# Four unused strips of 32 to 224 bytes that move where tiles begin in on-chip memory

## The chip, the cores and the metric

The kernel runs on one core of a Trainium2 chip. The metric is device time in microseconds (us) of one execution. Before the change, three runs gave a median of 1342.72 us (1341.16 to 1344.79). The profile is of one more execution of the same program.

The core has a matrix engine (PE; its weight loads are listed as PEld), a vector engine (DVE), an activation engine (ACT), GpSimd (POOL) and a queue engine (SP) that here only issues DMAs. On-chip memory has 128 partitions; "a tile begins at byte b" means byte b within every partition.

## The reference

One layer of a diffusion backbone over 256 latent tokens and 256 context tokens of width 2048, all in float32:

```python
h  = modulate(rmsnorm(x,  norm1_g), sh1, sc1)       # shifts and scales: silu(c) @ ada_w + ada_b
hc = modulate(rmsnorm(xc, norm1_g), csh1, csc1)
q, k, v, f, hy = split_projection(h @ w_in)         # 2048 -> 1024+1024+1024+512+1536
kc, vc = split(hc @ w_in[:, 1024:3072])
a = neighbourhood_attention(q, k, v, kc, vc, rpb)   # 8 heads of 128
y = merge_groups(a, fourier_mix(f), hyena_mix(hy, ...), mix_norm_g)
x = x + g1 * (y @ w_out)                            # 2048 x 2048
x = x + g2 * conv_gated_mlp(modulate(rmsnorm(x, norm2_g), sh2, sc2), ...)   # d_ff 5632
return rmsnorm(x, final_norm_g)
```

## The kernel before

Activations lie transposed: features on the 128 partitions, the 256 tokens along the row. A tile of 16 feature blocks is 16 rows of 256 float32, so one block is 1024 bytes in each partition.

**A main product takes three matmuls.** Weights and activations are split in two parts, hi (rounded to fp32r) and lo (the rest): `split` (L166) and `shift_split` (L238). `mm3` (L158) then adds hi·hi, hi·lo and lo·hi into one PSUM bank. Each of them is one MATMUL with one LDWEIGHTS ahead of it. The operand that is loaded by LDWEIGHTS is 128 columns (512 bytes) and is called stationary here; the operand that streams through is called moving. In the names of the profile the moving operand stands first: `acc_ps<-h_hi,w_hi` streams `h_hi` past a loaded `w_hi`.

In nearly all main products the activation is the moving operand, 256 columns or 1024 bytes of a row, and the weight is stationary. Only for the values of attention (the second half of `group`, L539) is it the other way: there a weight of 512 columns streams past a loaded activation.

**The weights** come from HBM in pieces of 128 x 1024 float32 into eight `raw` buffers (`Weights.load`, L248, on SP's queue), are split by ACT (hi) and DVE (lo) into two buffers each of `w_hi` and `w_lo`, and each such pair serves 48 matmuls (48 or 96 in the key and value stage). `Stream` (L272) asks for a chunk ahead of its use. Beside that, `pump` (L342) puts weight columns of the modulation through DVE (L333), in places given by a table.

**The stages**, in order:

- Key and value stage (L583 to L597): norms, the first modulation rows (L466, `s_t` stationary side of a small product), and keys and values of latent and context tokens. `group` alternates 48 matmuls on `hx_hi`, `hx_lo` (latent) with 48 on `hc_hi`, `hc_lo` (context), from the same weight buffers.
- Other input projections (L684 to L774): Fourier, Hyena and query columns, by `wide` on `hx_hi`, `hx_lo`, with the Fourier and Hyena mixing between them.
- Attention and output projection (L784 to L847): `yB_hi`, `yB_lo`, `yA_hi`, `yA_lo` are moving.
- Feed-forward part (L849 to L910): the up products on `h2_hi`, `h2_lo` (in the profile `h_hi`, `h_lo`), 4224 matmuls, and the down products on `yh`, `yl`, 2112 matmuls; then the last norm and the output.

**Where tiles lie.** Every pool is a contiguous piece of the partition. Pools on the right side are stacked downward from the top, so a strip in an early one moves every later one down too, until a pool is closed and its place given back. The `rot` pool at the top holds `hx_hi` (tag A, later `xr`), `kT` (tag C, later `h2_hi`) and `v_t` (tag D, later `h2_lo`). Below it lie, one after the other in time: `x_lo` (the tiles `hx_lo`), `hy`, `p1` (with `hc_hi`), `c_lo` (with `hc_lo`); later `fourier`, `hyena`, `att` (with `yA` and `yB`) and `ffn` (with `yh`, `yl`). The weight buffers lie on the left side.

Of the kernel before, what the change touches and what calls it, by code (L numbers as in the profile page):

```python
# [8 lines left out]
F32 = mybir.dt.float32  # L9
# [6 lines left out]
P = 128  # L16
# [19 lines left out]
for _n, _k in V_LAYOUT:  # L36
# [10 lines left out]
    p1=(0, 0, 2, 6, 9),  # L47
    blocks=(2, 2, 4, 4, 4),
    win=0.8,
    att=(1, 0, 1, 4, 0, 1, 0, 0),  # L50
# [12 lines left out]
    wa=(1, 2, 0, 0, 0, 1, 0, 0),  # L63
    outs=(2, 4, 4, 4, 2),
)


def kv_blocks():
# [55 lines left out]
def hybrid_block(ctx: ExitStack, tc: tile.TileContext, a: dict, out: bass.AP):  # L124
# [5 lines left out]
    def pool(stack, name, bufs=1, side=None, **kw):  # L130
        return stack.enter_context(tc.tile_pool(name=name, bufs=bufs, side=side, reuse_waits="tile", **kw))

    acc_ps = pool(ctx, "acc_ps", 5, space=PSUM)
    mi_ps = pool(ctx, "mi_ps", 3, space=PSUM)

    def bank(p=None):
        p = p or mi_ps
# [63 lines left out]
    def rms_bcast(pool_, sqs, n, name, ps=None):  # L201
        if ps is None:
            ps = bank()
            col_sums(ps, sqs)
        ms = pool_.tile([P, 2], F32, name=f"{name}_m", tag=f"{name}_m")
        TS(ms[:], ps[:, 0:2], 1.0 / n, EPS, op0=ALU.mult, op1=ALU.add)
        r = rstd_of(pool_, ms[:], 2, name)
        ps = bank()
        for t in range(2):
            dg = cst.tile([P, P], F32, tag="dg", name="dg", bufs=2)  # L210
            TS(dg[:], ident, r[:, t : t + 1], None, op0=ALU.mult)
            mm(ps[:, t * P : (t + 1) * P], ones[:], dg[:], True, True)
        rb = pool_.tile([P, L], F32, name=f"{name}_b", tag=f"{name}_b")
        nc.vector.tensor_copy(rb[:], ps[:, :L])
        return rb
# [73 lines left out]

    w1 = Weights(ctx, 8, 2)  # L290

    rot = pool(ctx, "rot", 1, "right")

    def rtile(tag, shape, dt, name):
# [57 lines left out]
    p1 = pool(p1s, "p1", 1, "right")  # L352
# [2 lines left out]
    s_t = p1.tile([P, KT, 32], F32, name="s_t")  # L355
    nc.gpsimd.memset(s_t[:], 0.0)
    hc_hi = p1.tile([P, KT, L], F32R, name="hc_hi")
    hc_lo = Pairs(c_pool, F32R, "hc_lo")
    hs = ((hx_hi, hx_lo), (hc_hi, hc_lo))
    xs = [Pairs(z, F32, "x_in", KT // 2) for z in (x_pool, c_pool)]  # L360
# [323 lines left out]
    with ExitStack() as st:  # L684
        fp = pool(st, "fourier", 1, "right")
# [98 lines left out]
    with ExitStack() as st:  # L784
        ap_ = pool(st, "att", 1, "right")
        yA_hi, yA_lo = (ap_.tile([P, 8, L], F32R, name=f"yA_{z}") for z in ("hi", "lo"))
        aT = ap_.tile([P, NH, L], F32, name="aT")
        yB_hi = ap_.tile([P, 8, L], F32R, name="yB_hi")
        yB_lo = ap_.tile([P, 8, L], F32R, name="yB_lo")
        for i in range(0, 8, 2):  # L790
            split(yB_hi[:, i : i + 2, :], yB_lo[:, i : i + 2, :], yB[:, i : i + 2, :])
        sqa = ap_.tile([P, L], F32, name="sqA")
        held = {}
        x_parts = []

        def wout_chunk(h, n, kc):
            yh, yl = ((yB_hi, yB_lo), (yA_hi, yA_lo))[h]
            if kc == 0:
                held[n] = [bank(acc_ps) for _ in range(2)]
            wide_chunk(stream, h * 8 + n * 2 + kc, held[n], yh, yl, kc * 4, kc == 0, kc == 1, h * kc == 1 and n == 3)  # L800
            if kc == 1:
                add_scaled(held[n], n, G1)
            if h == 1:
                pump(CFG["wa"][2 * n + kc])
            if h == 1 and kc == 1:
                square_parts(ap_, n, x_parts, "PT", 2)

        scale = 128.0 ** -0.5
        for hd in range(NH):
            PT = ap_.tile([P, 4, L], F32, tag="PT", name="PT", bufs=2)  # L810
            for t in range(2):
                ps = bank(acc_ps)
                mm(ps[:], qT[:, hd, t * P : (t + 1) * P], kT[:, hd, :], True, True)
                s = ap_.tile([P, 512], F32, tag="s", name="s", bufs=3)
                STT(s[:, :L], ps[:, :L], scale, bias[:, hd, 2 - 2 * t : 6 - 2 * t, :].rearrange("p m c -> p (m c)"), op0=ALU.mult, op1=ALU.add)
                nc.scalar.activation(s[:, L:], ps[:, L:], AF.Copy, scale=scale)
                sm = ap_.tile([P, 3], F32, tag="sm", name="sm", bufs=3)
                nc.vector.tensor_reduce(sm[:, 0:1], s[:], axis=AX.X, op=ALU.max, negate=True)
                nc.scalar.activation(s[:], s[:], AF.Exp, bias=sm[:, 0:1], accum_out=sm[:, 1:2])
                nc.vector.reciprocal(sm[:, 2:3], sm[:, 1:2])  # L820
                TS(s[:], s[:], sm[:, 2:3], None, op0=ALU.mult)
                ps = bank()
                for j in range(4):
                    transpose(ps[:, j * P : (j + 1) * P], s[:, j * P : (j + 1) * P])
                nc.scalar.copy(PT[:, :, t * P : (t + 1) * P], ps.rearrange("p (j n) -> p j n", n=P))  # L825
            ps = bank()
            for j in range(4):
                mm(ps[:, :L], v_t[:, j, hd * P : (hd + 1) * P], PT[:, j, :], j == 0, j == 3)
            nc.scalar.copy(flip(aT[:, hd, :]), ps[:, :L].rearrange("p (r c) -> p r c", c=GW))
            square_into(ap_, sqa, aT[:, hd, :], hd == 0)  # L830
            for c in range(CFG["pace"][hd], CFG["pace"][hd + 1]):
                wout_chunk(0, c // 2, c % 2)
            pump(CFG["att"][hd])
        group_norm(ap_, [aT[:, i, :] for i in range(NH)], V_MIX, yA_hi, yA_lo, 0, [sqa])
        for c in range(CFG["pace"][NH], 8):
            wout_chunk(0, c // 2, c % 2)
        for n in range(4):
            for kc in range(2):
                wout_chunk(1, n, kc)
        pump(CFG["rest"])  # L840
        rb2 = rms_bcast(ap_, x_parts, D, "r2")
        STT(A2[:], A2[:], 1.0, vec[:, V_N2 : V_N2 + KT], op0=ALU.add, op1=ALU.mult)
        h2_hi = rtile("C", [P, KT, L], F32R, "h2_hi")
        h2_lo = rtile("D", [P, KT, L], F32R, "h2_lo")
        for k in range(KT):
            t = modulate(ap_, xr[:, k, :], A2[:, k : k + 1], rb2[:])
            shift_split(t, B2[:, k : k + 1], h2_hi[:, k, :], h2_lo[:, k, :])  # L847
# [14 lines left out]
    for kind, g in plan:  # L862
        if kind == "up":
            if g == 0:
                pss = [bank(acc_ps) for _ in range(4)]
                for kc in range(4):
                    for m in range(2):
                        wide_chunk(stream, ci + 2 * kc + m, pss[2 * m : 2 * m + 2], h2_hi, h2_lo, kc * 4, kc == 0, kc == 3)
                gates, upps = pss[:2], pss[2:]
            else:  # L870
                gates = wide(stream, ci, h2_hi, h2_lo)
            gls = []
            for h in range(2):
                ga = fp.tile([P, 2, L], F32, tag="ga", name="ga", bufs=3)
                for i in range(2):
                    nt = g * 4 + 2 * h + i
                    wv = [vec[:, V_FCW + 44 * q + nt : V_FCW + 44 * q + nt + 1] for q in range(3)]
                    conv(gates[h][:, i * L : (i + 1) * L], ga[:, i, :], *wv, vec[:, V_FCB + nt : V_FCB + nt + 1])
                nc.scalar.activation(ga[:], ga[:], AF.Gelu_apprx_tanh)
                gls.append(ga)  # L880
            if g:
                upps = wide(stream, ci + 4, h2_hi, h2_lo)
            ci += 8
            yh = fp.tile([P, 4, L], F32R, tag="yh", name="yh", bufs=6)
            yl = fp.tile([P, 4, L], F32R, tag="yl", name="yl", bufs=6)
            for h in range(2):
                TT(gls[h][:], upps[h].rearrange("p (i n) -> p i n", n=L), gls[h][:], op=ALU.mult)
                split(yh[:, 2 * h : 2 * h + 2, :], yl[:, 2 * h : 2 * h + 2, :], gls[h][:])
            ys[g] = (yh, yl)
        else:  # L890
            if g == 0:
                pump(99)
            gs = halves[g]
            for n in range(4):
                pss = [bank(acc_ps) for _ in range(2)]
                for q in gs:
                    wide_chunk(stream, ci, pss, *ys[q], 0, q == gs[0], q == gs[-1], g == 1 and n == 3 and q == gs[-1])
                    ci += 1
                add_scaled(pss, n, G2)
                if g == 1:  # L900
                    square_parts(fp, n, f_parts, "ga2", 1)
                    for c in range(4 * n, 4 * n + 4):
                        nc.scalar.activation(xr[:, c, :], xr[:, c, :], AF.Copy, scale=vec[:, V_FG + c : V_FG + c + 1])
    rb = rms_bcast(fp, f_parts, D, "rf")
    c0 = 0
    for n in CFG["outs"]:
# [91 lines left out]
```

## Time and profile before

| | |
|---|---|
| median of three runs | 1342.72 us |
| the profiled execution | 1340.31 us |
| its span, first to last instruction | 1338.5 us |
| mean granted TensorE clock | 0.986 |
| PE busy | 1311.0 us, 10302 matmuls |
| DVE busy | 890.7 us |
| ACT busy | 555.7 us |
| mean rate of the DMAs | 234 GB/s |

A PE that is listed as busy says little here: a matmul of 256 columns is listed with about 280 ns, but the next begins after some 115 to 120 ns, since matmuls overlap. What counts is the time from the start of one matmul to the start of the next, called the interval below. It is read from the chain of work that ended last (a piece's length by its number of matmuls), from the timeline (starts of single matmuls), or from a stretch of time by the number of matmuls that touch it.

### The profile page before, as it was taken

Reading aid. Unit: us, or ns where it says so; the run is one execution under the profiler, and the core shown is the slowest. Engines: PE = TensorE matmul, PEld = TensorE weight load, DVE = VectorE, ACT = ScalarE, POOL = GpSimd, SP = SyncE. Lnnn points to the kernel's source line nnn. Section 1 sums busy time; section 2 is a strip of 40 time slices with the busy share of each in tenths; the row PEclk is TensorE's granted clock in tenths of the full one; section 3 lists DMA queues with packets and bytes.
Section 4 is the critical chain, followed back from the end, with each engine's and each line's share of the span. In section 5 each row is a group of like instructions: output and inputs, shape, how many; then the busy total and the mean of one; then the engine's idle time right before and its main releaser. Section 6 shows DMA issues by size and latency. Waiting matters only on the chain.

```text
span 1338.5 us, 24519 instructions
## 1 busy us (share of the span) xinstructions
PE 1311.0 (98%) x10302; PEld 1235.1 (92%) x10302; DVE 890.7 (67%) x1305; ACT 555.7 (42%) x735; POOL 0.9 (0%) x7
## 2 busy tenths in 40 slices
PE   9899999999999999989999999999999999999996
PEld 5677788899989889989999999999999999999996
DVE  5347668958999998877666767644445554555653
ACT  4252212135334665455443444333334443443542
POOL 0000000000000000000000000000000000000000
PEclk9799999999999999989999999999999999999997
DMA  8677888987669775746777777855555555565531
GB/s 322 248 303 284 329 325 306 339 274 275 214 235 343 286 232 184 275 139 223 251 245 260 246 246 248 280 183 186 189 188 189 190 186 192 184 194 183 188 135 64
DMA packets 93311, 313.18 MB, mean 234 GB/s; under 512 B 16016, under 2 KB 16272, under 8 KB 92816
## 3 DMA queue, kind: packets, MB, share of 16 engines
q1 hardware_dynamic: 92912, 311.07, 67.5%
q8 instruction: 80, 1.31, 0.4%
q10 hardware_dynamic: 288, 0.55, 0.1%
q14 instruction: 31, 0.25, 0.1%
HBM read 309.48 MB, written 2.10 MB: 233 GB/s over the span
## 4 chain that ended last, share of the span: by engine, by line
PE 94%; DVE 3%; DMA 1%; ACT 1%; issue 0%; DVEq 0%; ACTq 0%
PE acc_ps L156 87%; PE mi_ps L156 4%; PE mi_ps L466 2%; PE mi_ps L164 1%; DMA raw<-in_ada_col_t 1%; DVE w_lo L168 0%; DMA pack<-in_pack 0%; DVE xr L908 0%; ACT w_hi L167 0%; DVE raw L333 0%; DVE Y L731 0%; DVE rs_r L223 0%; ACT PT L825 0%; DVE u L659 0%; DVE gt L666 0%
## 5 line engine op out<-in xcount | busy, mean ns | idle before, releaser
L167 ACT CAST w_hi<-raw 128x1024 fp32r<-128x1024 f32 x376 | 380.6, 1049 | 565.3 <-PE acc_ps L156 490.1
L168 DVE TENSOR_TENSOR w_lo<-raw,w_hi 128x1024 fp32r<-128x1024 f32 x376 | 448.2, 1222 | 241.5 <-ACT w_hi L167 239.5
L156 PE MATMUL acc_ps<-h_hi,w_hi 128*128 128x256 f32 x1408 | 394.7, 281 | 1.6 <-ACT h_hi L239 1.6
L156 PE MATMUL acc_ps<-h_lo,w_hi 128*128 128x256 f32 x1408 | 394.7, 280 | 0.0
L156 PE MATMUL acc_ps<-h_hi,w_lo 128*128 128x256 f32 x1408 | 394.7, 280 | 0.0
L156 PEld LDWEIGHTS acc_ps<-h_hi,w_hi 128*128 128x128 f32 x1408 | 265.7, 189 | 1.8 <-ACT h_hi L239 1.8
L156 PEld LDWEIGHTS acc_ps<-h_lo,w_hi 128*128 128x128 f32 x1408 | 265.7, 189 | 0.0
L156 PEld LDWEIGHTS acc_ps<-h_hi,w_lo 128*128 128x128 f32 x1408 | 265.7, 189 | 0.0
L156 PE MATMUL acc_ps<-yh,w_lo 128*128 128x256 f32 x704 | 196.8, 280 | 0.0
L156 PE MATMUL acc_ps<-yl,w_hi 128*128 128x256 f32 x704 | 196.7, 279 | 0.0
L156 PE MATMUL acc_ps<-yh,w_hi 128*128 128x256 f32 x704 | 196.4, 279 | 0.0
L333 DVE SCALAR_TENSOR_TENSOR raw<-raw,s_row 128x1024 f32<-128x1024 f32 x128 | 154.8, 1223 | 44.2 <-DMA raw<-in_ada_col_t 39.6
L156 PE MATMUL acc_ps<-hx_hi,w_hi 128*128 128x256 f32 x512 | 145.0, 285 | 1.0 <-ACT hx_hi L239 1.0
L156 PE MATMUL acc_ps<-hx_lo,w_hi 128*128 128x256 f32 x512 | 144.8, 283 | 0.3 <-DVE hx_lo L240 0.3
L156 PE MATMUL acc_ps<-hx_hi,w_lo 128*128 128x256 f32 x512 | 144.0, 283 | 0.0
L156 PEld LDWEIGHTS acc_ps<-yl,w_hi 128*128 128x128 f32 x704 | 132.3, 188 | 0.0
L156 PEld LDWEIGHTS acc_ps<-yh,w_hi 128*128 128x128 f32 x704 | 132.0, 187 | 0.0
L156 PEld LDWEIGHTS acc_ps<-yh,w_lo 128*128 128x128 f32 x704 | 131.9, 187 | 0.0
L156 PEld LDWEIGHTS acc_ps<-hx_hi,w_hi 128*128 128x128 f32 x512 | 96.5, 189 | 6.6 <-ACT w_hi L167 2.5
L156 PEld LDWEIGHTS acc_ps<-hx_lo,w_hi 128*128 128x128 f32 x512 | 97.0, 190 | 1.5 <-issue 0.9
L156 PEld LDWEIGHTS acc_ps<-hx_hi,w_lo 128*128 128x128 f32 x512 | 96.7, 189 | 1.5 <-issue 1.5
L637 DVE SCALAR_TENSOR_TENSOR xr<-acc_ps,G,xr 128x256 f32<-128x256 f32 x64 | 27.0, 479 | 20.0 <-PE acc_ps L156 20.0
(227 smaller groups left out, 1534.5 us busy)
## 6 DMA issues: line engine op xcount, KB each, us to landing
raw<-in_ffn_t SPq DMA_DIRECT2D x264, 512.0 KB, 4.4
raw<-in_ada_col_t SPq DMA_DIRECT2D x128, 512.0 KB, 4.8
raw<-in_ada_t SPq DMA_DIRECT2D x64, 512.0 KB, 6.3
raw<-in_w_in_t SPq DMA_DIRECT2D x48, 512.0 KB, 5.4
raw<-in_w_kv_t SPq DMA_DIRECT2D x32, 512.0 KB, 6.0
raw<-in_w_out_t SPq DMA_DIRECT2D x32, 512.0 KB, 4.5
x_in<-in_xT SPq DMA_DIRECT2D x8, 256.0 KB, 5.6
x_in<-in_cT SPq DMA_DIRECT2D x8, 256.0 KB, 7.1
```

The source lines that it names most:

```text
L156: nc.tensor.matmul(ps, lhsT, rhs, start=start, stop=stop, skip_group_check=True)
L164: nc.tensor.transpose(ps, src, ident[:n, :n])
L167: nc.scalar.copy(hi, src)
L168: TT(lo, src, hi.bitcast(F32), op=ALU.subtract)
L333: STT(r, r, 1.0, s_row[:, h * NA : (h + 1) * NA], op0=ALU.mult, op1=ALU.mult, accum_out=sums_[:, f, h : h + 1])
L466: nc.tensor.matmul(ps[32 * j : 32 * j + 32, :w], s_t[:, kt, :], raws[(kt - n2 * q) // (n2 // 2)][:, kt % (n2 // 2), :], start=kt < 4, stop ...
L637: STT(xr[:, c, :], pss[nt // 2][:, (nt % 2) * L : (nt % 2 + 1) * L], cols[:, c : c + 1], xr[:, c, :], op0=ALU.mult, op1=ALU.add)
```

## The change

Four tiles that nobody writes or reads are added, each a strip of unused bytes:

- 224 bytes in a pool of its own ahead of `rot`, which moves `rot` and all pools on the right side down by 224;
- 32 bytes at the end of `p1`;
- 224 bytes in `att`, behind `sqA`;
- 160 bytes in `ffn`, ahead of the last norm's tiles.

```diff
+PADS = {"edge": 224, "p1": 32, "att": 224, "ffn": 160}
...
+    def pad(pool_, nbytes):
+        pool_.tile([P, nbytes // 4], F32, name="pad")
...
     w1 = Weights(ctx, 8, 2)
 
+    pad(pool(ctx, "edge", 1, "right"), PADS["edge"])
     rot = pool(ctx, "rot", 1, "right")
...
     hc_hi = p1.tile([P, KT, L], F32R, name="hc_hi")
+    pad(p1, PADS["p1"])
     hc_lo = Pairs(c_pool, F32R, "hc_lo")
...
         sqa = ap_.tile([P, L], F32, name="sqA")
+        pad(ap_, PADS["att"])
         held = {}
...
+    pad(fp, PADS["ffn"])
     rb = rms_bcast(fp, f_parts, D, "rf")
```

No instruction is added, removed or moved: on each engine and queue the instructions of the two programs stand in the same order, with the same waits. Only addresses differ. These are the first bytes of the tiles in the two programs, with the remainder by 256:

| tiles | role | before | mod 256 | after | mod 256 |
|---|---|---|---|---|---|
| `hx_hi` (later `xr`) | moving; stationary for values | 180192 | 224 | 179968 | 0 |
| `hx_lo` (first of 8) | the same | 163808 | 224 | 163584 | 0 |
| `hc_hi` | the same | 118528 | 0 | 118272 | 0 |
| `hc_lo` (lowest of its places) | the same | 100096 | 0 | 99840 | 0 |
| `yA_hi`, `yA_lo`, `yB_hi`, `yB_lo` | moving | 114368 and on | 192 | 113920 and on | 0 |
| `h2_hi` (earlier `kT`) | moving | 196576 | 224 | 196352 | 0 |
| `h2_lo` (earlier `v_t`) | moving | 212960 | 224 | 212736 | 0 |
| `yh`, `yl` (first of 6 each) | moving | 123776, 148352 | 128 | 123392, 147968 | 0 |
| `w_hi`, `w_lo` (two each) | stationary; moving for values | 46912 to 71488 | 64 | the same | 64 |
| `raw` | weights as loaded | 14144 and on | 64 | the same | 64 |
| Fourier's and Hyena's tiles | smaller float32 products | 109440 and on | 128 | 109216 and on | 160 |
| `PT`, `s` of attention | smaller float32 products | 156352, 164544 | 192 | 156128, 164320 | 224 |
| `qT`, `yB`, `bias` | on the left side | 79680 and on | 64 | the same | 64 |

Every block of a moving tile keeps its tile's remainder, since a block is 1024 bytes; each 128 columns of a weight keep theirs, since they are 512 bytes.

## The prediction

> **What bounds the kernel now.** I read the page first, then the chain of waits in order of time, then the timeline of PE where the two kinds of tiles meet, then stretches of time by their number of matmuls. The page's busy times and its chain by engine and by line:
>
> ```profile
> PE 1311.0 (98%) x10302; PEld 1235.1 (92%) x10302; DVE 890.7 (67%) x1305; ACT 555.7 (42%) x735; POOL 0.9 (0%) x7
> PE 94%; DVE 3%; DMA 1%; ACT 1%; issue 0%; DVEq 0%; ACTq 0%
> ```
>
> The matrix engine carries 94% of the chain that sets the end, so the interval from one matmul to the next sets the time. Two pieces of that chain are longer than all others:
>
> ```profile
> 212.52 77.37 PE acc_ps L156 x524
> 575.37 746.96 PE acc_ps L156 x6336
> ```
>
> The second is the whole feed-forward part, in one piece: 746.96 / 6336 = 117.9 ns a matmul, with nothing that PE waited for. What the others do there shows whether they could follow a faster PE (columns: stretch, busy time and number of instructions of PE, PEld, DVE, ACT, POOL, granted clock, DMA share, GB/s):
>
> ```profile
> 230.00:575.00 345.00, 337.94 (x2506) 315.78 (x2505) 302.77 (x500) 152.85 (x229) 0.00 (x0) 0.99 0.76 264
> 575.00:1338.00 763.00, 750.49 (x6360) 750.02 (x6360) 449.29 (x541) 327.67 (x390) 0.00 (x0) 0.99 0.61 201
> ACT w_hi L167 <- PE acc_ps L156: 490.1, 135, 12.5
> PE mi_ps L156 <- DVE X L738: 3.3, 1, 3.3
> ```
>
> In the feed-forward part (second row) DVE is busy 449 of 763 us and the DMA engines 0.61. The third row, from the list of who waited for whom, says that ACT stood 490 us in all until PE gave weight buffers back: the supply runs ahead of PE. From 230 to 575 us (first row) DVE is busy 303 of 345 us, and PE once waits 3.3 us for it (last row). There a faster PE may meet another limit.
>
> **What the trace says of where a tile begins.** The context tiles `hc_hi` and `hc_lo` already begin at a multiple of 256 bytes, with the weights at 64 behind one, and they alternate with the latent tiles `hx` (224 behind one) from the same weight buffers. PE's timeline holds the comparison, at full granted clock (start, length as listed, instruction):
>
> ```profile
> 212.83 0.39 PE L156 MATMUL acc_ps<-w_hi,hx_hi 128*128 128x512 f32 x1
> ...
> 217.03 0.40 PE L156 MATMUL acc_ps<-w_hi,hc_hi 128*128 128x512 f32 x1
> ...
> 222.54 0.28 PE L156 MATMUL acc_ps<-hx_hi,w_hi 128*128 128x256 f32 x1
> ...
> 228.23 0.28 PE L156 MATMUL acc_ps<-hc_hi,w_hi 128*128 128x256 f32 x1
> ...
> 233.68 0.28 PE L156 MATMUL acc_ps<-hx_hi,w_hi 128*128 128x256 f32 x1
> ```
>
> From 222.54 to 228.23 lie 48 matmuls with `hx` moving: 5.69 / 48 = 118.5 ns. From 228.23 to 233.68 lie 48 with `hc` moving: 5.45 / 48 = 113.5 ns. Operation, width, weights and clock are the same; only the activation tiles differ. With the activation stationary and 512 weight columns moving, 18 matmuls on `hx` take 4.20 us (212.83 to 217.03), or 233.3 ns each, and 24 on `hc` 5.51 us (217.03 to 222.54), or 229.6 ns.
>
> Other starts, by stretches of PE alone (stretch, busy time and number of matmuls that touch it, clock, DMA share, GB/s). A matmul is listed with 0.28 us, so the number belongs to the stretch plus 0.28 us:
>
> ```profile
> 530.00:568.00 38.00, 38.00 (x323) 1.00 0.79 272
> 600.00:840.00 240.00, 240.00 (x2048) 1.00 0.74 245
> 850.00:980.00 130.00, 130.00 (x1106) 1.00 0.59 196
> 990.00:1200.00 210.00, 210.00 (x1792) 1.00 0.58 188
> 1215.00:1320.00 105.00, 105.00 (x894) 1.00 0.44 146
> ```
>
> - `yA` (192 behind a multiple of 256): 38.28 / 323 = 118.5 ns.
> - `h2` (224 behind): 240.28 / 2048 and 210.28 / 1792, both 117.3 ns.
> - `yh`, `yl` (128 behind): 130.28 / 1106 and 105.28 / 894, both 117.8 ns.
>
> So three other remainders, under four different loads, give 117.3 to 118.5 ns; only remainder 0 gives 113.5. After the change all moving activations have remainder 0 and the weights keep 64, the pair that `hc` shows. I take 113.5 ns for all of them.
>
> By the Trainium skill, the expectation is another one. "TensorE: Matmul & The Clock Gate", section "Back-to-back issue gap", gives a warm interval of N/2.4 + 2.5 ns, from the columns alone: 109.2 ns for 256 columns, whatever the address. "SBUF — State Buffer", in the note on cachelines under "Door 1", has lines of 16 bytes, and all the remainders here (0, 64, 128, 192, 224) are multiples of 16. By either, the change does nothing. The trace has two intervals for one width, so the first is not the whole of it; what the two would make of the time stands among the rivals.
>
> **The change part by part.** Nothing is computed in the strips, and all engines and queues keep their order, so every term is a number of matmuls (counted in the code: a weight chunk of 4 x 512 serves 48) by a difference of intervals.
>
> - Up products, 88 chunks: 4224 x (117.3 - 113.5) = 16.1 us.
> - Down products, 44 chunks: 2112 x (117.8 - 113.5) = 9.1 us. Together 25.2 us, and PE's chain is unbroken there, so I take all of it.
> - Key and value stage: `hx` moving for keys, 8 chunks, 384 x (118.5 - 113.5) = 1.9 us; stationary for values, 192 x (233.3 - 229.6) = 0.7 us.
> - Other input projections, 24 chunks: 1152 on `hx`, x 5.0 = 5.8 us.
> - Output projection, 16 chunks: 768 on `yA`, `yB`, x (118.5 - 113.5) = 3.8 us.
>
> The last three lines make 12.2 us ahead of the feed-forward part, and here PE isn't alone. What can hold it back shows in the chain around 370 us:
>
> ```profile
> 351.26 15.82 PE acc_ps L156 x135
> 367.08 1.22 DVE w_lo L168 x2
> ...
> 372.81 6.74 DMA raw<-in_ada_col_t
> ...
> 395.23 5.61 PE mi_ps L156 x32
> 529.32 39.56 PE acc_ps L156 x331
> ```
>
> From 367.08 to 395.23 the end is set by DVE's queue and one landing of modulation columns, while PE still has work; the 3.3 us in which PE waits for L738 end at 395.23. The bounds are 0 (DVE and the DMAs fix all the points at which PE is released) and 12.2 us (PE sets them all). DVE is busy 88% of that stretch, near full but not full; I take the middle, 6 us.
>
> The other tiles that move are read and written by DVE and ACT, or are moving operands of plain float32 products. DVE and ACT don't show where a tile begins (behind the first bar: busy us, mean ns of one):
>
> ```profile
> L239 ACT ACTIVATE hc_hi<-ht,B 128x256 fp32r<-128x256 f32 x16 | 7.3, 505 | 8.7 <-DVE ht L235 8.7
> L239 ACT ACTIVATE hx_hi<-ht,B 128x256 fp32r<-128x256 f32 x16 | 7.3, 504 | 9.0 <-DVE B L480 5.6 <-DVE ht L235 3.4
> L240 DVE SCALAR_TENSOR_TENSOR hc_lo<-ht,B,hc_hi 128x256 fp32r<-128x256 f32 x16 | 7.1, 485 | 0.7 <-ACT hc_hi L239 0.7
> L240 DVE SCALAR_TENSOR_TENSOR hx_lo<-ht,B,hx_hi 128x256 fp32r<-128x256 f32 x16 | 7.0, 481 | 1.0 <-ACT hx_hi L239 1.0
> ```
>
> Remainder 0 takes 505 and 485 ns, remainder 224 takes 504 and 481: no term. The float32 products of Fourier, Hyena and attention go from remainders 128 and 192 to 160 and 224, none of them to 0. The page puts 4% of the chain on them:
>
> ```profile
> PE acc_ps L156 87%; PE mi_ps L156 4%; PE mi_ps L466 2%; PE mi_ps L164 1%; DMA raw<-in_ada_col_t 1%; DVE w_lo L168 0%; DMA pack<-in_pack 0%; DVE xr L908 0%; ACT w_hi L167 0%; DVE raw L333 0%; DVE Y L731 0%; DVE rs_r L223 0%; ACT PT L825 0%; DVE u L659 0%; DVE gt L666 0%
> ```
>
> 4% of 1338.5 is 54 us; if their starts mattered as much as `hx` against `hc` (4.4%), that would be 2.4 us either way. I take 0, since the remainders with a loss in the rows above differ by 1% only.
>
> Sum: 25.2 + 6 = 31.2 us. The profiled execution took 1340.31 us (its span 1338.5 and 1.8 around it), so 1309.1; the median of the runs shown lies 2.4 us above that execution. On the median: 1342.7 - 31.2 = 1311.5 us.
>
> **The rivals.**
>
> 1. *All of it counts.* PE fixes its own points of release before 575 us as well: 25.2 + 12.2 = 37.4, 1305.3 us. For it: ACT's 490 us of waiting for PE. Against: the 28 us from 367.08 to 395.23.
>
> 2. *Remainder 0 is not enough.* Counted by 512 bytes, `hc` lies at 256 and the weights at 320. After the change `hx`, `yA`, `yB` and `h2` also lie at 256, but `yh` and `yl` at 0. If the distance to the weights is what counts, the down products keep 117.8 ns and 9.1 us are missing: 22.1 saved, 1320.6 us. No row shows that distance; `hc` itself moves to 0 by 512, so it would slow down too. Against it: a moving row of 1024 bytes passes all remainders by 512.
>
> 3. *Nothing changes.* Something else makes `hc` fast, such as which region of the partition it lies in: 1342.7 us. For it: the two sections of the skill cited above. Against it: `yh` lies at 123776 to 148352, over much of `hc_hi`'s bytes (118528 to 134912), and shows 117.8 ns.
>
> 4. *Slower.* The interval comes from a clash between the two reads of PE, set by distances that no row shows, and the new ones are as bad as the worst row, 118.5 ns: 4224 x 1.2 + 2112 x 0.7 = 6.5 us lost in the feed-forward part, 1349.2 us. It decides from a mean interval in that part of 118.2 ns on, where 0.3% (4 us over 6336 matmuls) is lost. Against it: the pair 0 and 64 is shown by `hc`, at 113.5.
>
> **How the numbers follow.** My forecast (113 to 114 ns in the feed-forward part and part of the rest) has 0.70, rival 1 0.10, rival 2 0.08, rival 3 0.07, rival 4 0.05. The predicted time is the forecast's, 1311.5 us. Its own bounds: 0 to 12.2 us of the early stages give 1317.5 and 1305.3; half a nanosecond off the interval of 113.5 moves 3 us. The range is 1303 to 1324, which takes in rival 2. What a measurement of this kernel can tell from no change is about 0.3%, 4 us. Forecast and rivals 1 and 2 are faster by more: 0.88; rival 3 is the same: 0.07; rival 4 is slower: 0.05.
>
> **What would show it.** In the chain of the changed kernel, the piece of 6336 matmuls should be about 722 us long instead of 746.96. The stretches of the up and of the down products should both come to 113 to 114 ns; down products alone at 117 to 118 mean rival 2, both unchanged mean rival 3. In the timeline, `hx` and `hc` should have the same interval; `hc` should stay at 113.5. Ahead of the feed-forward part, the start of the long piece (575.37 now) should come 2 to 10 us earlier, and PE's wait for L738 should grow beyond 3.3 us if DVE takes the rest. The prediction is wrong if the long piece stays above 735 us, or if intervals reach 114 and the time doesn't follow since PE begins to wait for weights in the feed-forward part.

## The result, and the profile after

The changed kernel takes 1309.35 us (median of four executions; 1307.02 to 1338.39), the kernel before 1341.94: a ratio of 0.9752, with a 95% interval of 0.9726 to 0.9779. The ratio leaves out executions over 1.5% above the fastest of their kernel, but here the profiled one of these shows the kernel itself running at another rate, so they have to be told: of six executions of the changed kernel four took 1307 to 1311 us, one 1329.0 and one 1338.4.

The one that was profiled is that of 1338.4. From its chain of work that ended last, in order of time (start, length, piece), and from PE's stretches (stretch, busy time and number of matmuls that touch it, granted clock, DMA share, GB/s):

```profile
212.00 77.31 PE acc_ps L162 x524
572.69 748.24 PE acc_ps L162 x6336
```

```profile
120.00:128.00 8.00, 8.00 (x73) 1.00 0.70 270
222.00:233.00 11.00, 11.00 (x96) 1.00 0.68 257
532.00:552.00 20.00, 20.00 (x179) 1.00 0.77 283
600.00:840.00 240.00, 240.00 (x2040) 1.00 0.75 247
850.00:980.00 130.00, 130.00 (x1106) 1.00 0.58 189
```

As in the prediction, the number of matmuls belongs to the stretch plus 0.28 us. From 120 to 128 us the interval is 8.28 / 73 = 113.4 ns, from 532 to 552 (output projection) 20.28 / 179 = 113.3: that is what was forecast. But from 222 to 233 it is 11.28 / 96 = 117.5, and in the feed-forward part 240.28 / 2040 = 117.8 (up) and 130.28 / 1106 = 117.8 (down), at full clock, in one unbroken piece, with every tile where the change puts it. So one pair of remainders shows two intervals, 113.3 and 117.8 ns. The difference of 4.5 ns, over 6336 matmuls, is some 28 us; this execution lies 28 to 31 us above the four short ones.

The trace of the kernel before shows the second interval too, in a place that the prediction didn't read. There a stretch of 24 matmuls on the context tiles, at a granted clock of 1.00, begins and ends with these:

```profile
96.89 0.28 PE L156 MATMUL acc_ps<-hc_hi,w_hi 128*128 128x256 f32 x1
99.59 0.28 PE L156 MATMUL acc_ps<-hc_hi,w_lo 128*128 128x256 f32 x1
```

That is 23 intervals in 2.70 us, 117.4 ns, with tiles and weights at the remainders (0 and 64) that show 113.5 ns at 228 us. Of the ten stretches of this kind nine come to 113 to 114 ns after some matmuls, and this one doesn't.

Ahead of the feed-forward part the gain is small: the long piece begins at 572.69 us instead of 575.37, 2.7 us earlier. PE's longest waits:

```profile
PE mi_ps L162 <- DVE dg L217: 7.2, 4, 2.7
PE mi_ps L162 <- DVE X L746: 4.1, 1, 4.1
```

The wait for the last step of the long convolution (L738 before, L746 now) grew from 3.3 to 4.1 us, so DVE takes some of the gain, as forecast.

### The profile page after: what moved, and what is told of

Same layout as the page of the kernel before. It is cut to its first block, busy times and chain, and to the rows that moved or that the text cites. A ratio compares the mean times of both kernels' runs of the same rounds, so it can differ in the third digit from the quotient of the medians.

```text
span 1336.6 us, 24519 instructions
## 1 busy us (share of the span) xinstructions
PE 1307.4 (98%) x10302; PEld 1231.2 (92%) x10302; DVE 889.7 (67%) x1305; ACT 554.7 (42%) x735; POOL 0.9 (0%) x7
## 4 chain that ended last, share of the span: by engine, by line
PE 88%; DVE 7%; DMA 2%; ACT 1%; issue 1%; SPq 0%; DVEq 0%; ACTq 0%
PE acc_ps L162 80%; PE mi_ps L162 4%; PE mi_ps L474 2%; DVE w_lo L174 2%; DMA raw<-in_ada_col_t 1%; DVE raw L340 1%; PE mi_ps L170 1%; DMA raw<-in_w_out_t 1%; ACT w_hi L173 1%; DMA raw<-in_ada_t 1%; DVE xr L645 0%; DMA pack<-in_pack 0%; DVE Y L739 0%; DVE xr L918 0%; DVE X L184 0%
## 5 line engine op out<-in xcount | busy, mean ns | idle before, releaser
L162 PEld LDWEIGHTS acc_ps<-h_hi,w_hi 128*128 128x128 f32 x1408 | 271.0, 193 | 1.9 <-ACT h_hi L245 1.9
L162 PEld LDWEIGHTS acc_ps<-yh,w_hi 128*128 128x128 f32 x704 | 135.2, 192 | 0.0
L665 ACT ACTIVATE ga<-acc_ps,pack 128x256 f32<-128x256 f32 x44 | 23.7, 559 | 39.3 <-PE acc_ps L162 33.7
```

The costliest lines, as they stand in the source:

```text
L162: nc.tensor.matmul(ps, lhsT, rhs, start=start, stop=stop, skip_group_check=True)
L665: nc.scalar.activation(dst, ps, AF.Identity, bias=b, scale=w1_)
```

## The experiments

Two questions were open: what sets the interval, the moving tile's remainder or its distance to the weights; and why one program runs in two ways. *Distance* is how many bytes the weights' start lies behind the moving tile's, modulo 256: 64 in the change; before, 96 for `hx` and `h2`, 192 for `yh` and `yl`, 128 for `yA` and `yB`, 64 for `hc`.

### The change once more

The same program, without an edit.

> The changed kernel once more, for a second profile of it. The profiled execution that came with the result has the piece of 6336 feed-forward matmuls at 748.24 us, 118.1 ns each, though its tiles begin at multiples of 256; in other stages the same execution shows 113.3 ns. Theory A (two intervals): with these addresses an unbroken stretch of matmuls holds either about 113.3 or about 117.8 ns, whichever it falls into at its start, and keeps it. Then most executions are near 1308 with the long piece at 718 to 721 us, and some are 20 to 29 us longer with all or part of that piece at 117.8. Theory B (the address fixes the interval): every execution has the long piece at 718 to 722, and the execution of 1338 had another cause, which would show in waits or clock.

Five executions: 1308.24, 1310.32, 1323.63, 1337.44, 1338.33 us. The profiled one (1338.33) again has the long piece at 117.8:

```profile
572.77 748.11 PE acc_ps L162 x6336
```

It is one unbroken piece of PE's own work, so theory B has no wait to name. Theory A stands, though three of these five executions are long, where it expected most near 1308; the next run shows the other interval.

### The same distance at other remainders

```diff
-PADS = {"edge": 224, "p1": 32, "att": 224, "ffn": 160}
+PADS = {"edge": 96, "p1": 32, "att": 224, "ffn": 160}
...
             self.raw = pool(stack, "w_raw", nraw, side)
+            pad(pool(stack, "w_edge", 1, side), 128)
             self.sp = pool(stack, "w_split", nsp, side)
```

> The distance of the change at another place: moving tiles all at remainder 128, weights all at 192 (64 behind them). Theory 1 and theory 3 (the moving tile must begin at a multiple of 256): 117.3 to 118.5 ns everywhere, as the down products had at 128, so about 1340 us or some us more, since the context tiles lose their place too. Theory 2 (distance alone): as the change, 113.3 ns and 1309 us.

All tiles on the right side and the weights lie 128 bytes higher than in the change. A ratio of 0.9744 (0.9714 to 0.9773); three executions at 1306.7 to 1309.6 us and one of 1339.49. From the chain and PE's stretches of the profiled one (1309.56 us):

```profile
571.45 257.62 PE acc_ps L162 x2258
829.08 462.48 PE acc_ps L162 x4078
```

```profile
538.00:558.00 20.00, 20.00 (x172) 1.00 0.78 265
600.00:820.00 220.00, 220.00 (x1944) 1.00 0.76 256
860.00:960.00 100.00, 100.00 (x885) 1.00 0.59 196
```

The up products take 220.28 / 1944 = 113.3 ns, the down products 100.28 / 885 = 113.3, with no moving tile at a multiple of 256; the output projection ahead of them shows the other interval, 20.28 / 172 = 117.9. The remainder of the moving tile by itself isn't what counts; theories 1 and 3 fall. The feed-forward part, 746.96 us before, lasts 720.1 (829.08 + 462.48 - 571.45).

### Two other distances with the moving tiles at 0

Weights at remainder 0 (a strip of 192 bytes, shown) and at remainder 128 (a strip of 64 in the same place):

```diff
             self.raw = pool(stack, "w_raw", nraw, side)
+            pad(pool(stack, "w_edge", 1, side), 192)
             self.sp = pool(stack, "w_split", nsp, side)
```

> As the change, and a strip of 192 bytes ahead of the weights' split buffers: weights begin at a multiple of 256 too (remainder 0 beside 0). Theory 1 (only the moving tile's remainder counts): 113.3 ns as with 64, 1309 us. Theory 2 (the distance between the two operands counts): distance 0 is a new one, and the interval differs from 113.3 by some ns, 6 us of the whole per ns. Theory 3 (every 256-byte boundary that an operand crosses costs some 4 ns): weights of 512 bytes cross one less, about 109 to 110 ns, 1285 us.

> As the change, with weights at remainder 128 instead of 64 (a strip of 64 bytes ahead of the split buffers). Theory 1: 113.3 ns, 1309 us. Theory 2: an interval other than 113.3 in the long piece (117 or more would put it at 1335 to 1345). Theory 3: 113.3, since the number of boundaries is that of 64.

Both are slower than the kernel before, though every moving activation begins at a multiple of 256: ratios of 1.0098 (1.0070 to 1.0126) and 1.0069 (1.0047 to 1.0092). Feed-forward stretches of the first, then of the second:

```profile
600.00:820.00 220.00, 220.00 (x1836) 1.00 0.72 241
860.00:960.00 100.00, 100.00 (x835) 1.00 0.54 182
```

```profile
600.00:820.00 220.00, 220.00 (x1836) 1.00 0.72 240
860.00:960.00 100.00, 100.00 (x836) 1.00 0.56 189
```

220.28 / 1836 is 120.0 ns in both, and the down products agree: more than any stage of the kernel before shows. The moving tiles lie as in the change and only the weights moved, so with the run above the distance (theory 2) is what separates 113.3 from 120.0. Fewer 256-byte boundaries in the weights gained nothing.

A distance of 128 isn't tied to 120.0, though: the output projection has it in the kernel before (118.5 ns) and in this second run, where its stretch gives 18.28 / 154 = 118.7 ns:

```profile
537.00:555.00 18.00, 18.00 (x154) 1.00 0.80 290
```

The profiled execution of that run, 1358.14 us, is the longest of ten; seven lie at 1347.6 to 1350.5. By an estimate from these rows, feed-forward products at 118.5 to 118.7 ns would take 8 to 10 us less, about the difference; no such execution was profiled.

### Three more distances, dealt out to the stages in two ways

The first has the up products at 32, the down products at 224 and the output projection at 160; the second, with strips of 128, 32, 32 and 96 bytes, has them at 224, 160 and 32.

```diff
-PADS = {"edge": 224, "p1": 32, "att": 224, "ffn": 160}
+PADS = {"edge": 192, "p1": 32, "att": 96, "ffn": 96}
```

> Other distances, the weights left at remainder 64: up products, projections and context at distance 32 (moving at 32), output projection at 160 (moving at 160), down products at 224 (moving at 96). Distance means how far the weights' start lies behind the moving tile's, modulo 256. Known so far: 0 and 128 give 120.0 ns, 64 gives 113.3 or 117.8, 96 gave 117.3 and 192 gave 117.8 in the kernel before. Theory M (it counts modulo 128, so 160 is as 32 and 224 as 96): 224 gives 117.3 in the down products, and 32 and 160 are equal. Theory N (only 64 to either side of a clash, modulo 256): all three between 117 and 120, no run under 1335 us.

> The same three distances dealt out otherwise: up products, projections and context at 224 (moving at 96), output projection at 32 (moving at 32), down products at 160 (moving at 160). Both theories expect each distance to show the interval that it shows in the other kernel, whatever the stage; theory M 117.3 for the up products, theory N 117 to 120 throughout. If a distance shows two intervals by stage, the stage or the history counts beside the distance.

1.0016 (0.9999 to 1.0032) and 1.0025 (1.0007 to 1.0043): no gain, within what can be told from no change. Up and down stretches of the first (its third row is the second half of the down products), then of the second:

```profile
600.00:820.00 220.00, 220.00 (x1861) 1.00 0.73 244
860.00:960.00 100.00, 100.00 (x860) 1.00 0.57 189
1220.00:1300.00 80.00, 80.00 (x681) 1.00 0.55 185
```

```profile
600.00:820.00 220.00, 220.00 (x1870) 1.00 0.72 245
860.00:960.00 100.00, 100.00 (x836) 1.00 0.55 182
```

Distance 32 gives 118.4 ns and 160 gives 120.0, so theory M falls as it stood. 224 gives 117.8 in the up products of the second run, and in the down products of the first both 116.6 and, later in the same execution, 80.28 / 681 = 117.9: with one distance and one stage, something else counts too, as with 64. Theory N holds here but for the 116.6; the distance scan below ends it.

### One part of the change undone

The down products' tiles back at remainder 128, distance 192:

```diff
-PADS = {"edge": 224, "p1": 32, "att": 224, "ffn": 160}
+PADS = {"edge": 224, "p1": 32, "att": 224, "ffn": 32}
```

> One part of the change undone: yh and yl back at remainder 128 (distance 192), the rest as changed. By the terms of the prediction the down products go back to 117.8 ns and 9 us are lost: fast executions near 1317. Theory M: 192 is the same as 64, so the down products keep the interval in which the up products ran (113.3 in fast executions, then 1308), and 117.8 before was the slower of the two intervals. Theory N: 117.8 in the down products whatever the up products do.

Four executions, 1317.56 to 1320.27 us; ratio 0.9832 (0.9804 to 0.9860). Against the short executions of the change (1307.0 to 1310.6) some 10 us are lost, where the prediction's term for the down products says 9.1. The stretches of up, down, up and down in turn:

```profile
600.00:820.00 220.00, 220.00 (x1943) 1.00 0.75 256
840.00:960.00 120.00, 120.00 (x1021) 1.00 0.58 191
980.00:1180.00 200.00, 200.00 (x1767) 1.00 0.60 193
1195.00:1295.00 100.00, 100.00 (x852) 1.00 0.45 148
```

113.4, 117.8, 113.3, 117.7 ns: the interval changes with the distance from stage to stage, and the second up stage came back to 113.3 behind a stage at 117.8. Theory M expected 113.3 in the down products and 1308 us, so it falls here too.

### Extra matmuls to shift the stretch

If a stretch keeps the interval into which it falls, something foreign in it might shift it to the shorter one. Twelve matmuls, twice, in the first up group:

```diff
+    def kick(wh, src, n):
+        ps = bank()
+        for _ in range(n):
+            mm(ps[:, :L], wh[:, 3, :P], src.rearrange("p k n -> p (k n)")[:, 56 : 56 + L], True, True)
...
-                        wide_chunk(stream, ci + 2 * kc + m, pss[2 * m : 2 * m + 2], h2_hi, h2_lo, kc * 4, kc == 0, kc == 3)
+                        wide_chunk(stream, ci + 2 * kc + m, pss[2 * m : 2 * m + 2], h2_hi, h2_lo, kc * 4, kc == 0, kc == 3, kicks=12 * (m == 1 and kc in (1, 3)))
```

> As the change, and twice in the first up group (behind its 2nd and its last chunk) 12 extra matmuls whose moving operand begins at remainder 224, as the tiles of the kernel before; their sums are not used. In the kernel before, the context tiles always came to 113.3 ns a few matmuls after such ones, in 12 of 12 stretches. Theory A (two intervals, kept by an unbroken stretch until something shifts it): the extra matmuls cost 24 x 0.117 = 2.8 us and shift the stretch to 113.3 every time, so all executions lie at 1308 to 1313, none at 1325 to 1340. Theory A' (the shift is by chance): executions near 1311 and near 1340 as before. Theory B (the slow executions come from elsewhere, such as the DMAs): the slow ones stay as frequent, 3 us later.

Six executions: 1310.48, 1311.62, 1314.66, 1330.79, 1338.53, 1340.48 us. Stretches of the first, ahead of the first place, between the two, and behind the second:

```profile
575.00:592.00 17.00, 17.00 (x152) 1.00 0.56 170
595.00:617.00 22.00, 22.00 (x189) 1.00 0.65 218
625.00:825.00 200.00, 200.00 (x1767) 1.00 0.76 258
```

113.7, 117.9 and 113.3 ns: the stretch shifts where the extra matmuls stand, the first time to the longer interval, the second time back. The tiles, the weight buffers and the granted clock (1.00) are the same in all three rows. That shows the two intervals in one stretch. The extra matmuls don't always shift it to the shorter one, and three of the six executions are long, so theory A' stands, by chance as far as can be seen.

What was expected of this run calls the context tiles of the kernel before fast in 12 of 12 stretches; its trace has ten, and in one of them, shown with the result, they stay at 117.4 ns.

The same with a distance of 192 (`32 : 32 + L` in place of `56 : 56 + L`):

> As the run with 12 extra matmuls in two places of the first up group, but their moving operand begins at remainder 128, a distance of 192 to the weights, instead of 224. With extra matmuls at 96, one place took the stretch from 113.3 to 117.8 and the next took it back, so that distance throws the stretch by chance. In the kernel with the down products at 192, the up products behind them came to 113.3 at once, and none of its 4 executions was slow. Theory C (from a distance of 192 a stretch at 64 always begins at 113.3): all executions lie at 1309 to 1314, none over 1320. Theory A' (chance): about a third lie 20 us higher, as without the extra matmuls.

1311.08, 1311.55, 1313.24, 1313.32, 1339.98 and 1341.61 us: two of six are long, so theory C falls and A' stands. In the profiled execution (1313.24) the stretch was at the shorter interval ahead of both places, between them and behind them, so how two others came to 1340 wasn't seen:

```profile
580.00:592.00 12.00, 12.00 (x108) 1.00 0.52 166
600.00:618.00 18.00, 18.00 (x161) 1.00 0.70 231
630.00:830.00 200.00, 200.00 (x1767) 1.00 0.77 259
```

These are 113.7, 113.5 and 113.3 ns.

### The interval by distance

```diff
+D_UP = (64, 32, 40, 48, 56, 60, 68, 72, 80, 88, 52)
+D_DOWN = (16, 112, 144, 176, 208, 240, 192, 64)
...
+        sh = (64 - d) % 256 // 4
...
+            k = min(k, src.shape[1] - 2)
+            return src.rearrange("p k n -> p (k n)")[:, k * L + sh : (k + 1) * L + sh]
```

> A measurement of the interval alone: as the change, but in the feed-forward part the moving operand of each group is read from some bytes further on in the same tile, so that the distance to the weights is 64, 32, 40, 48, 56, 60, 68, 72, 80, 88, 52 in the eleven up groups (384 matmuls each), and 16, 112, 144, 176, 208, 240, 192, 64 in the eight parts of the down products (288 or 240 each). It multiplies other numbers than the kernel should in that part; number and size of all instructions are kept. Theory R (the interval depends on the distance in steps of 32 or 64 bytes): 40 to 60 show one value, 68 to 88 another. Theory S (it depends on the distance itself): a smooth course with its least near 64. Theory U (64 is one point of a rule by 16-byte lines): 48, 64, 80 are alike and those between are slower. If a distance shows 109 to 112 ns, it beats the change by 6 us per ns.

The weights stay at remainder 64 here, so distance and remainder of the moving tile change together.

One profile, PE's stretches inside each group (distances in the kernel's order: 64, 32, 40, 48, 56, 60 up; 16, 112, 144, 176 down; 68, 72, 80, 88, 52 up; 208, 240, 192, 64 down):

```profile
595.00:615.00 20.00, 20.00 (x179) 1.00 0.73 239
620.00:660.00 40.00, 40.00 (x340) 1.00 0.72 239
666.00:706.00 40.00, 40.00 (x333) 1.00 0.71 239
712.00:752.00 40.00, 40.00 (x345) 1.00 0.78 260
757.00:797.00 40.00, 40.00 (x335) 1.00 0.74 241
803.00:843.00 40.00, 40.00 (x336) 1.00 0.74 248
850.00:878.00 28.00, 28.00 (x241) 1.00 0.61 194
884.00:912.00 28.00, 28.00 (x239) 1.00 0.53 181
920.00:945.00 25.00, 25.00 (x223) 1.00 0.53 177
950.00:979.00 29.00, 29.00 (x244) 1.00 0.55 182
985.00:1025.00 40.00, 40.00 (x337) 1.00 0.57 185
1031.00:1071.00 40.00, 40.00 (x335) 1.00 0.58 181
1076.00:1116.00 40.00, 40.00 (x338) 1.00 0.56 185
1122.00:1162.00 40.00, 40.00 (x337) 1.00 0.58 183
1168.00:1208.00 40.00, 40.00 (x336) 1.00 0.57 184
1214.00:1238.00 24.00, 24.00 (x205) 1.00 0.57 193
1243.00:1266.00 23.00, 23.00 (x199) 1.00 0.59 192
1270.00:1293.00 23.00, 23.00 (x205) 1.00 0.61 192
1297.00:1320.00 23.00, 23.00 (x198) 1.00 0.00 1
```

| distance | ns | distance | ns | distance | ns |
|---|---|---|---|---|---|
| 16 | 117.3 | 60 | 119.9 | 112 | 118.3 |
| 32 | 118.5 | **64** | **113.3**, 117.6 | **144** | **113.4** |
| 48 | 116.8 | 68 | 119.5 | 176 | 120.0 |
| 52 | 119.9 | 72 | 120.2 | **192** | **113.6** |
| 56 | 120.2 | 80 | 119.2 | 208 | 118.4 |
| 40 | 121.0 | 88 | 119.5 | 240 | 117.0 |

Each value is one stretch in one execution; one matmul more or less in the number moves it by 0.3 to 0.6 ns, and at distances with two intervals it shows one of them. The course isn't smooth: four bytes to either side of 64 lose 6 ns against its shorter interval. So theory S falls; theory R falls too, since 40 to 60 spread from 116.8 to 121.0, and theory U, since 48, 64 and 80 are not alike. No distance comes under 113.3. Three show 113.3 to 113.6: 64, 192 and 144; that ends theory N. Of these 192 showed 117.8 in the kernel before and with one part undone, so it has two intervals as well; 64 shows both in this one profile (first and last row).

### All of the last two stages at a distance of 144

Each moving tile of the output projection and the feed-forward part is made 256 bytes longer and used from byte 176 on (shown for `h2_hi`; the same for `h2_lo`, `yA`, `yB`, `yh` and `yl`, and `kT` and `v_t`, which share tags C and D, are made as long):

```diff
+    def late(tile_, k):
+        return tile_[:, 44 : 44 + k * L].rearrange("p (k n) -> p k n", n=L)
...
-        h2_hi = rtile("C", [P, KT, L], F32R, "h2_hi")
+        h2_hi = late(rtile("C", [P, KT * L + 64], F32R, "h2_hi"), KT)
...
```

> The feed-forward part and the output projection at a distance of 144: yA, yB, h2, yh and yl begin at remainder 176 inside tiles that are 256 bytes longer, weights at 64; latent and context tiles stay at 0. In the scan, 144 showed 113.3 ns after a few matmuls, entered from a stretch without a fixed interval. Theory D (144 has one interval): all executions near 1308, none slow, and the long piece at 718 to 721 us in each. Theory A at 144 too (two intervals, 113.3 and a slower one): some executions 20 to 30 us longer, as with 64. If the scan's stretch was short enough to mislead, all executions lie at 1335 or more.

> The kernel with the distance of 144 once more, to tell chance from a rule: none of its 6 executions was slow, where 11 of 27 of the kernels with a distance of 64 in the feed-forward part were. Theory D (144 has one interval): again all at 1307 to 1312. Theory A (it has two as well, and 6 were luck, with a chance of 0.59 to the 6th, 4%): about two of six at 1325 to 1340.

Eleven executions in the two runs, all between 1305.42 and 1310.64 us; ratios 0.9766 (0.9739 to 0.9792) and 0.9756 (0.9737 to 0.9776). The long piece in the two profiles, first run and second, and PE's wait for the long convolution in the first:

```profile
570.85 721.32 PE acc_ps L165 x6336
PE mi_ps L165 <- DVE X L749: 4.5, 1, 4.5
```

```profile
569.26 720.80 PE acc_ps L165 x6336
```

By time these are the change's short executions, but none was long. Among the five kernels' runs above that have a distance of 64 through the whole feed-forward part (the change in two runs, the one with other remainders, and the two with extra matmuls), 11 of 27 executions lay at 1323 us or above; if 144 behaved so, and each execution fell by itself, 11 short ones in a row would have a chance of 0.59 to the 11th, 0.3%. This version is as fast as the change at its best, and didn't fall back in these eleven. That 144 has no second interval is not shown beyond these eleven.

## Why the prediction was right, and where its steps failed

- **The time.** 1311.5 was forecast, 1309.35 came out; the range holds it. The feed-forward term holds for the short executions. Feed-forward part: 25.2 us forecast; where its interval was 113.3 ns, the piece fell from 746.96 to 720.1 (same distance, other remainders) and 720.8 and 721.3 us (144), so 26 to 27 us. Its share of the down products, 9.1, is the 10 us lost when that part was undone.
- **Ahead of the feed-forward part.** 6 us, the middle of 0 and 12.2, was the term with the least ground. The long piece began at 575.37 before; it began at 572.69 and 572.77 in the two profiles of the change, at 571.45 at other remainders and, in the two runs at 144, at 570.85 and 569.26: 2.6 to 6.1 us, so 6 was at the upper end. Rival 1 (all 12 us) shows in none of them, and PE's wait for the long convolution grew from 3.3 to between 3.8 and 4.5 us, as the prediction said it would if DVE takes the rest.
- **"Only remainder 0 gives 113.5."** The reason was wrong, though the pair (0, 64) was right. Remainder 128 with weights at 192 gives 113.3, and remainder 0 with weights at 0 or 128 gives 120.0. In the trace of before, remainder and distance went together, since the weights lay at 64 throughout; `hc` against `hx` couldn't separate them. The working took the remainder for the cause in its words while it used the pair in its sum.
- **"I take 113.5 ns for all of them."** The step that failed in the profile: it took an interval that 48 matmuls showed for a property of the addresses. A distance of 64 has two, 113.3 and 117.8 ns, and a stretch of 6336 matmuls can hold the longer one from end to end. The trace of before warned of it twice: `hc` at 97 us stayed at 117.4 ns, and the prediction's own rows have 118.5 ns for `hx` and 117.3 for `h2`, at the same remainder 224. The prediction named "above 735 us" for the long piece as what would prove it wrong; two profiled executions have 748. `hc`, which "should stay at 113.5", shared the 117.5 ns from 222 to 233 us. That the median came out as forecast is luck in part: four of six executions fell into the shorter interval, and the same program once more, with two of five, had a median of 1323.63 us.
- **Rival 2 (the distance counts).** It was the right cause with the wrong modulus. Counted by 512, `h2` (64) and `yh` (320) differ in the change and in the run with other remainders; in each of the profiles both show the same interval, 113.3 in the latter. That the distance repeats by 128 is excluded as well: 32 and 160 gave 118.4 and 120.0.
- **Rival 4 (distances that no row shows can be worse than the worst row).** Not the case for the change, but a worse interval exists: 120.0 ns, at a distance of 0, which no row before showed, and at 128, which the output projection had shown at 118.5, made two kernels slower by 1.0 and 0.7%. That the two reads of PE clash isn't shown.
- **The rules of the skill.** The Trainium skill's "TensorE: Matmul & The Clock Gate", section "Back-to-back issue gap", gives N/2.4 + 2.5 ns, 109.2 ns for 256 columns, as the gap of an isolated matmul. For a stream of LDWEIGHTS and MATMUL pairs, as here, the same section has measured figures at 128 and 512 columns only, which the prediction left unsaid. No distance of the scan came under 113.3, and the intervals spread from 113.3 to 121.0 at one width and full clock. The Trainium skill's note on cachelines in "SBUF — State Buffer", "Door 1", has lines of 16 bytes. If only the place within such a line counted, 48, 64 and 80 would be alike; they gave 116.8, 113.3 and 119.2. Here the measurement decides against both as the whole account.
- **The smaller terms** (DVE and ACT untouched by remainders, float32 products without a term) were not tested by themselves. Behind the start of the long piece there is no room for them: in the run with other remainders the profiled execution is 30.75 us shorter than that of before, and 3.92 us of earlier start and 26.85 us of the long piece make 30.77. Ahead of it they can't be told from the rest of the 2.6 to 6.1 us.

## What to carry to other kernels

Where matmuls follow each other without a gap, read their interval from starts, not from busy time, and sort it by operand: a few per cent between equal shapes point to where the operands lie. Here the distance between the moving operand and the weights decides which intervals can occur: moving both by 128 bytes kept the 113.3 ns, and moving the weights alone lost it. A natural comparison in one trace doesn't tell remainder from distance; move both by the same amount before believing either. A gain found in a short stretch should be looked for in several whole executions, since the same program can hold one of two rates for its whole length.

## What wasn't expected

- One pair of addresses with two intervals, 113.3 and 117.8 ns, each kept for hundreds to thousands of matmuls at full clock, and switched both ways by twelve foreign matmuls. What makes the choice at the start of a stretch stays open. It isn't taken over from the stage ahead: in the first profile of the change the output projection ran at 113.3 and the feed-forward part at 117.8, and at other remainders the output projection ran at 117.9 and the feed-forward part at 113.3. The feed-forward part begins at a granted clock of 0.50 in every profile kept, which may set it, but no run varied that.
- How sharp the dependence is: 119.9 ns at a distance of 60, 113.3 at 64, 119.5 at 68. No rule was found that gives 64, 144 and 192 together. What in the chip the distance stands for isn't shown.
